# Twelve of 22 feature tiles joint in a macaron block's FFNs; GpSimd splits the last pair's sums; the mixers' first steps come later

## The chip, the cores and the metric

The kernel runs on one core of one Trainium2 chip. The metric is the device time of one execution in microseconds (us). Before the change the median of three runs is 2143.7 us (2139.63 to 2148.18). TensorE (PE) does the matmuls, VectorE (DVE), ScalarE (ACT) and GpSimd (POOL) the elementwise work, SyncE (SP) issues most of the transfers.

## The reference, cut to what matters

The block has 1024 rows of width 1024, all in fp32. Both FFNs have a hidden width of 2816, that is 22 tiles of 128 features.

```python
x = x + 0.5 * _swiglu(_rms_norm(x, ffn1_norm), ffn1_w_gate, ffn1_w_up, ffn1_w_down)
h = _rms_norm(x, mix_norm)
proj = h @ w_in
mixed = concatenate([gla_mixer(proj[:, :GLA_PROJ]), rwkv7_mixer(proj[:, GLA_PROJ:])])
x = x + mixed @ w_out
x = x + 0.5 * _swiglu(_rms_norm(x, ffn2_norm), ffn2_w_gate, ffn2_w_up, ffn2_w_down)
return _rms_norm(x, final_norm)
# _swiglu(h, g, u, d) = (silu(h @ g) * (h @ u)) @ d
```

## The kernel before

The rows are worked on in two halves, A and B, of 512. Every fp32 operand is split into a rounded high part and the rest (`halved`, `stage`, `stage_f`: a cast on ACT, then a subtraction on DVE), and every product is three matmuls: high by high, high by low, low by high (`mm3`). All of them are recorded at line 43; a full one has 512 columns.

**The two kinds of FFN tiles.** Tiles 0 to 11 (`NS` is 12) are done for each half apart in `ffn`: `pgu` is the product with the gate and up weights, `pdn` that with the down weights. Tiles from `NS` on are joint: A and B together, in pairs of tiles, by a scheme with 7 products in place of 8. `joint_up` (`pju`) makes the hidden blocks; at the end of each pair it puts seven operands, named by their product 1 to 7, split, into DRAM (`put`, the transfer at L829). Four of them are sums that GpSimd makes (L833, L835, L838, L842). `joint_down` (`pjd`) then runs the products in the order 1, 6, 2, 7, 5, 4, 3, in each over all pairs. It loads the hidden operand (`hh<-d_hid`), the down weights (`wdk`, loaded with product 1 and kept), forms the weight sums of products 6, 7, 5 and 4 on GpSimd (L864 to L870, into slots of the tile `EG`) and splits them. The results leave PSUM as running sums in the first four slots of `EG` and as additions to the residual rows `x`.

**The order of the stages** is FFN1 of A (tiles per half), joint FFN1, projections and mixers of A, out-projection of A, the same for B, FFN2 of B's first tiles, joint FFN2, final norms and FFN2 of B's other tiles. `mixers` runs the GLA units (`gla_unit`: `pkv`, `pA`, `pB`, `po`) and the RWKV units (`pg`, `p`, `p1b`, `p2b`, `pav`, `pz`, `pu`, `px`, `py`, `pyT`) as streams of small matmuls. Between them it takes fillers from a generator: FFN1 of B beside A's mixers, FFN2 of A beside B's. Each stream yields the nanoseconds from `LAT` that it wants to stay away from PE; it comes back when that has passed in the planner's clock, and for the time placed `FILL` sets how many fillers go in. TensorE's order in there is the one written. The fillers stop at `AFTER`, and what is left of the generator runs as `run(f1b, n=3)` before the out-projection (`pout`) and as `run(f1b)` behind it. The other engines' instructions are ordered by a scheduler at build time.

**Around the change.** Before `pout`, `outprep` loads the mixers' output from DRAM (`xnL<-d_mix`), casts it on ACT (L1285) and subtracts on DVE (L1286). What stands between the last `py` and that: a copy of `py` to `AV` (ACT), a group norm over it (L226 to L233, DVE), a transpose (`pyT`, L46), a scaling (`AV<-pyT`, L244, ACT), an addition and a product (L248, DVE), and the store `d_mix<-AV`.

Of the kernel before, what the change touches and what calls it, by code (L numbers as in the profile page):

```python
# [5 lines left out]
CDEC=float(np.exp(-0.5))  # L6
MULT,ADD,SUB,MAX,MIN=ALU.mult,ALU.add,ALU.subtract,ALU.max,ALU.min

LAT=dict(pre=3000,gram=0,c32=3000,inv2=1400,D=900,m1=900,m2=900,x2=700,pav=900,w=600,z=1000,u=1000,x=1500,gn=6000,gpre=2635,lev0=5723,lev=1944,sc=770,on=8372)

def const_array():
    p=np.arange(128)
# [239 lines left out]
def gla_unit(g, p, src, vsrc, gsrc, mixouts):  # L252
# [10 lines left out]
    fr=[slice(0,64),slice(64,128)]  # L263
    c4=lambda t: t.rearrange("p (c t)->p c t",t=128)
    el=g.el[p]
    yield LAT["gpre"]
    pkv=ps("pkv")
    for c in range(4):
        for h in range(2):
# [83 lines left out]
P = 128  # L353
D = 1024
# [3 lines left out]
DFF = 2816  # L358
NF = DFF // P

NS = 12
PAIRS = [(f, f + 1) for f in range(NS, NF, 2)]
THREES = [list(range(f, min(f + 3, NS))) for f in range(0, NS, 3)]
AFTER = ("gu", len(THREES) - 1, THREES[-1][0])
TWOS = [list(range(f, min(f + 2, NS))) for f in range(0, NS, 2)]
CUT = 6
# [26 lines left out]
def block_kernel(tc, ctx, x, consts, coff, vecs, finaln, wgu, wdn, win_t, win_v, w_out, alw, wa2, g2, out):  # L393
# [300 lines left out]
    def halved(f, H, L):  # L694
        S.copy(H, f)  # L695
        V.tensor_tensor(L, f, H.bitcast(F32), op=SUB)  # L696
# [61 lines left out]
    def joint_up(w, X, ep, spare):  # L758


        def tmp(nm):
            return ep.tile([P, HT], F32, tag="e", bufs=11, name=nm)

        def left(f1, f2, m):

            raw = {(i, kh): stage_load(wgu[w][(f * 2 + m) * 2 + kh]) for kh in range(2) for i, f in ((1, f1), (2, f2))}
            yield 1, stage_f(raw[1, 0])
            s1 = ep.tile([P, HT], F32, tag="s", bufs=3, name="s1")
            GP.tensor_tensor(s1, raw[2, 0], raw[2, 1], op=ADD)
            s2 = ep.tile([P, HT], F32, tag="s", bufs=3, name="s2")  # L770
            GP.tensor_tensor(s2, s1, raw[1, 0], op=SUB)
            yield 6, stage_f(s2)
            yield 2, stage_f(raw[1, 1])
            s3 = ep.tile([P, HT], F32, tag="s", bufs=3, name="s3")
            GP.tensor_tensor(s3, raw[1, 0], raw[2, 0], op=SUB)
            yield 7, stage_f(s3)
            yield 5, stage_f(s1)
            yield 4, stage_f(raw[2, 1])
            GP.tensor_tensor(s2, raw[1, 1], s2, op=SUB)
            yield 3, stage_f(s2)  # L780

        for j, (f1, f2) in enumerate(PAIRS):
            gate, over = {}, {}
            for m in range(2):
                C = {}
                for i, u in left(f1, f2, m):
                    ps = pm.tile([P, HT], F32, tag="pm", name="pju") if i in (6, 7, 4) else pa.tile([P, HT], F32, tag="pa", name="pju")
                    for q in range(4):
                        sl = slice(P * q, P * q + P)
                        xo = (X[i][0][:, q], X[i][1][:, q])  # L790
                        mm3(ps, (u[0][:, sl], u[1][:, sl]), xo, q == 0, q == 3)
                    if i == 1:
                        C[1, 1] = p1 = tmp("p1")
                        S.copy(p1, ps)
                    elif i == 6:
                        C[1, 2] = u2 = tmp("u2")
                        V.tensor_tensor(u2, ps, p1, op=ADD)
                    elif i == 2:
                        V.tensor_tensor(p1, ps, p1, op=ADD)
                    elif i == 7:  # L800
                        C[2, 1] = tmp("u3")
                        V.tensor_tensor(C[2, 1], ps, u2, op=ADD)
                    elif i == 5:
                        C[2, 2] = tmp("c22")
                        V.tensor_tensor(C[2, 2], ps, C[2, 1], op=ADD)
                        V.tensor_tensor(u2, ps, u2, op=ADD)
                    elif i == 4:
                        V.tensor_tensor(C[2, 1], C[2, 1], ps, op=SUB)
                    else:
                        V.tensor_tensor(u2, ps, u2, op=ADD)  # L810
                    for key in {2: [(1, 1)], 5: [(2, 2)], 4: [(2, 1)], 3: [(1, 2)]}.get(i, []):
                        if m == 0:
                            gate[key] = C[key]
                            S.activation(C[key], C[key], AF.Silu)
                        else:
                            V.tensor_tensor(gate[key], C[key], gate[key], op=MULT)

            a11, a12, a21, a22 = gate[1, 1], gate[2, 1], gate[1, 2], gate[2, 2]

            def put(op, f):  # L820
                k = [6, 2, 7, 5].index(op) if j == len(PAIRS) - 1 and op not in (1, 3, 4) else None
                if k is None:
                    hh = ep.tile([P, 2, HT], F32R, tag="hh", bufs=3, name="hh")
                else:
                    if k % 2 == 0:
                        over[k] = spare[0].tile([P, 4, HT], F32R, tag=spare[1][k // 2], name="hhl")
                    hh = over[k // 2 * 2][:, 2 * (k % 2):2 * (k % 2) + 2]
                halved(f, hh[:, 0], hh[:, 1])
                nc.gpsimd.dma_start(hid_dram(w, j, op), hh.bitcast(F32).rearrange("p a t->p (a t)"))  # L829

            put(1, a11)
            s1 = tmp("s1")
            GP.tensor_tensor(s1, a21, a22, op=ADD)  # L833
            s2 = tmp("s2")
            GP.tensor_tensor(s2, s1, a11, op=SUB)  # L835
            put(6, s2)
            put(2, a12)
            GP.tensor_tensor(a11, a11, a21, op=SUB)  # L838
            put(7, a11)
            put(5, s1)  # L840
            put(4, a22)
            GP.tensor_tensor(s2, a12, s2, op=SUB)  # L842
            put(3, s2)

    def joint_down(w, c1, c2, ep, hold, between, first=None, early=False):
# [6 lines left out]
        def right(i, j):  # L852
# [6 lines left out]
            lo0, hi0, lo1, hi1 = kept[j]  # L859
            if i in (1, 2, 3):  # L860
                return stage_f({1: lo0, 2: lo1, 3: hi1}[i])
            t = EG[:, 5 + next(turn) % 3]
            if i == 5:
                GP.tensor_tensor(t, hi0, lo0, op=SUB)  # L864
            else:
# [8 lines left out]
            return [(pa if 4 * k + t < 5 else pm).tile([P, HT], F32, tag="pa" if 4 * k + t < 5 else "pm", name="pjd") for t in range(4)]  # L874

        def sums():
            return ep.tile([P, 8, HT], F32, tag="EG", name="EG")

        turn = iter(range(1000))
        EG = sums() if early else None  # L880
        for i in ORDER:
# [7 lines left out]
                    mm3(ps[t], (hh[:, 0, to], hh[:, 1, to]), u, j == 0, j == n - 1)  # L889
            EG = EG or sums()  # L890
            E = [EG[:, t] for t in range(4)]
            Gs = EG[:, 4]
            for t in range(4):
                def add(x, v, k=0.5):
                    V.scalar_tensor_tensor(x, v, k, x, op0=MULT, op1=ADD)
# [13 lines left out]
                        between[6](E[t][:, 0:1])  # L909
                elif i == 2:  # L910
                    add(x1[:, d1], ps[t])
                elif i == 7:
                    V.tensor_tensor(Gs, ps[t], E[t], op=ADD)
                    add(x2[:, d1], Gs)
                    add(x2[:, d2], Gs)
                    if t == 3 and i in between:
                        between[i](Gs[:, 0:1])
                elif i == 5:
                    add(x2[:, d2], ps[t])
                    add(x1[:, d2], ps[t])  # L920
                    add(x1[:, d2], E[t])
                    if t == 3 and i in between:
                        between[i](x1[:, 0:1])
                elif i == 4:
# [473 lines left out]
    def first(j):  # L1398
        if j < 4 and j % 2 == 0:
            front[j] = B.pool.tile([P, 4, HT], F32R, tag=XN[j // 2], name="hhf")  # L1400
        return front[j // 2 * 2][:, 2 * (j % 2):2 * (j % 2) + 2] if j < 4 else ep.tile([P, 2, HT], F32R, tag="hh", bufs=6, name="hh")

    joint_down(0, A, B, ep, lambda j: wide(A.pool, XN[j]) if j < 4 else wide(ep, "wd"),
               {1: load(A, xsp(A)), 6: load(B, xin(B)), 7: lambda gate: from_store(B, 0, gate), 5: lambda gate: from_store(B, 1, gate)}, first, True)
    from_store_split(B)
    ecm.__exit__(None, None, None)
# [142 lines left out]
```

## Time and profile before

| | |
|---|---|
| median of three runs | 2143.7 us |
| the profiled execution | 2152.21 us |
| its span, first to last instruction | 2150.4 us |
| TensorE busy | 2056.5 us, 96% of the span, 13588 matmuls |
| VectorE, ScalarE, GpSimd busy | 1451.6, 910.6, 469.0 us |
| mean granted TensorE clock | 0.982 |

A matmul on the page is counted busy from its start to its modelled end, and the next one starts before that. So the price of one is the distance of two starts, or the length of a piece in the chain of work that ended last by its count. In brackets behind a row stand the idle time of the engine just before it and what ended it. The profiled execution is 8.5 us above the median.

### The profile page before, as it was taken

The page shows a single profiled execution, that of the slowest core. Times are in us where ns is not written, and L with a number is a line of the kernel's source. Part 1 is how long each engine was busy: PE and PEld are TensorE (multiplying, and loading weights), DVE is VectorE, ACT ScalarE, POOL GpSimd, SP SyncE. Part 2 cuts the span into 40 slices and gives each one's busy share as a digit, 9 for nine tenths or more (in the row PEclk, how much of TensorE's full clock was granted, in tenths as well). Part 3 has the DMA queues.
Part 4 walks back from the last instruction along what each step waited for, and adds up shares of the span by engine and source line. Part 5 has one row for each costly group of instructions (what it writes and reads, how often), then busy time and mean ns, then how long its engine had stood idle before and what let it go on. Part 6 is the DMA issues. An engine that isn't in the chain of part 4 may idle for free. (4 is left out here: it accounts for less than half of the span.)

```text
span 2150.4 us, 36294 instructions
## 1 busy us (share of the span) xinstructions
PE 2056.5 (96%) x13588; PEld 1643.0 (76%) x13588; DVE 1451.6 (68%) x3031; ACT 910.6 (42%) x1703; POOL 469.0 (22%) x490
## 2 busy tenths in 40 slices
PE   8999999978999999999999989999999999988998
PEld 7778788756888777777878867777777878877886
DVE  6675578738659578765575956876668458876755
ACT  6432234322465545354265644535434223432243
POOL 0410364446012300000001220001113036445400
PEclk9999999989999999999999999999999999999999
DMA  5333334676355744324336674442534333459442
GB/s 192 128 118 94 107 133 166 227 274 233 124 196 192 246 136 139 117 81 163 103 123 195 196 254 114 133 119 90 184 101 146 98 103 142 157 192 366 169 139 74
DMA packets 172639, 336.82 MB, mean 157 GB/s; under 512 B 17296, under 2 KB 56240, under 8 KB 172464
## 3 DMA queue, kind: packets, MB, share of 16 engines
q1 hardware_dynamic: 147328, 250.08, 35.9%
q0 software_dynamic: 21536, 73.41, 9.3%
q10 hardware_dynamic: 3600, 11.01, 1.4%
q8 instruction: 107, 1.75, 0.3%
q14 instruction: 68, 0.56, 0.1%
HBM read 242.17 MB, written 92.27 MB: 156 GB/s over the span
## 5 line engine op out<-in xcount | busy, mean ns | idle before, releaser
L460 DVE TENSOR_TENSOR wL<-raw,wH 128x512 fp32r<-128x512 f32 (+1 forms) x430 | 296.5, 697 | 277.7 <-ACT wH L459 275.4
L459 ACT CAST wH<-raw 128x512 fp32r<-128x512 f32 (+1 forms) x430 | 264.2, 619 | 478.2 <-PE pgu L43 161.2
L43 PE MATMUL pgu<-xnH,wH 128*128 128x512 f32 (+1 forms) x784 | 311.8, 398 | 0.1
L43 PE MATMUL pgu<-xnL,wH 128*128 128x512 f32 (+1 forms) x784 | 311.0, 397 | 0.0
L43 PE MATMUL pgu<-xnH,wL 128*128 128x512 f32 (+1 forms) x784 | 309.7, 396 | 0.2 <-DVE wL L460 0.2
L43 PE MATMUL pju<-T,wH 128*128 128x512 f32 x640 | 200.6, 394 | 2.4 <-ACT wH L695 2.4
L43 PE MATMUL pjd<-wH,hh 128*128 128x512 f32 x528 | 169.8, 402 | 24.5 <-ACT wH L695 20.9
L43 PEld LDWEIGHTS pgu<-xnH,wH 128*128 128x128 f32 x784 | 148.6, 190 | 33.5 <-ACT xnH L518 0.5
L43 PEld LDWEIGHTS pgu<-xnH,wL 128*128 128x128 f32 x784 | 148.9, 190 | 33.0 <-DVE wL L460 0.4
L43 PEld LDWEIGHTS pgu<-xnL,wH 128*128 128x128 f32 x784 | 148.9, 190 | 32.5 <-issue 0.7
L43 PE MATMUL pdn<-wH,hH 128*128 128x512 f32 x384 | 155.1, 406 | 6.8 <-ACT silu L665 3.7
L43 PE MATMUL pdn<-wL,hH 128*128 128x512 f32 x384 | 155.7, 406 | 2.4 <-DVE wL L460 2.4
L43 PE MATMUL pdn<-wH,hL 128*128 128x512 f32 x384 | 154.8, 404 | 0.4 <-DVE hL L672 0.4
L631 DVE SCALAR_TENSOR_TENSOR x<-pdn,x 128x512 f32<-128x512 f32 x152 | 104.3, 688 | 65.7 <-PE pdn L43 64.4
L43 PEld LDWEIGHTS pju<-T,wH 128*128 128x128 f32 x640 | 120.2, 188 | 31.1 <-ACT wH L695 3.3
L43 PE MATMUL pp<-xnH,wH 128*128 128x512 f32 x352 | 140.8, 400 | 0.0
L43 PEld LDWEIGHTS pjd<-wH,hh 128*128 128x128 f32 x528 | 101.8, 193 | 49.5 <-ACT wH L695 21.7
L43 PE MATMUL pp<-xnL,wH 128*128 128x512 f32 x352 | 139.0, 395 | 0.0
L43 PE MATMUL pp<-xnH,wL 128*128 128x512 f32 x352 | 138.7, 394 | 0.0
L43 PE MATMUL pju<-T,wL 128*128 128x512 f32 x320 | 126.2, 394 | 0.0
L43 PE MATMUL pjd<-wL,hh 128*128 128x512 f32 x264 | 106.4, 403 | 7.2 <-DVE wL L696 7.2
L696 DVE TENSOR_TENSOR wL<-s,wH 128x512 fp32r<-128x512 f32 x80 | 68.3, 855 | 42.5 <-ACT wH L695 42.5
(395 smaller groups left out, 4127.8 us busy)
## 6 DMA issues: line engine op xcount, KB each, us to landing
raw<-in_wgu_dram SPq DMA_DIRECT2D x272, 256.0 KB, 2.7
hh<-d_hid SPq DMA_DIRECT2D x66, 512.0 KB, 4.6
d_hid<-hh POOLq DMA_DIRECT2D x62, 512.0 KB, 3.7
raw<-in_wdn_dram SPq DMA_DIRECT2D x96, 256.0 KB, 2.6
raw<-in_win_t_dram SPq DMA_DIRECT2D x88, 256.0 KB, 2.9
d_x<-x SPq DMA_DIRECT2D x20, 512.0 KB, 2.9
wdk<-in_wdn_dram SPq DMA_DIRECT2D x20, 512.0 KB, 7.7
raw<-in_w_out_dram SPq DMA_DIRECT2D x32, 256.0 KB, 2.8
```

Source lines behind the costliest of these rows:

```text
L43: return self.t.matmul(out,lhsT,rhs,**kw)
L459: S.copy(H, raw)
L460: V.tensor_tensor(L, raw, H.bitcast(F32), op=SUB)
L631: V.scalar_tensor_tensor(h.x[tt][:, co], ps, 0.5, h.x[tt][:, co], op0=MULT, op1=ADD)
L696: V.tensor_tensor(L, f, H.bitcast(F32), op=SUB)
```

## The change

`NS` goes from 12 to 10, so six pairs (tiles 10 to 21) are joint in both FFNs and ten tiles are done per half. `put` gets another order (1, 2, 4, 6, 7, 5, 3), and for the last pair the four GpSimd sums (6, 7, 5, 3) go to spare tiles and are split by GpSimd itself, with a cast and a subtraction. In `joint_down` `EG` has seven slots in place of eight: the running sum of product 7 is written over the one before it, and its eight additions to `x` come after all four PSUM reads; the additions of product 6's running sum move from product 5 to product 2. In the joint FFN1 the weights of the fifth and sixth pair have tiles of their own. In `LAT`, `pre` goes from 3000 to 8000, and the first GLA unit waits 8000 where it waited 2635. Lines from L829 on move by 4 or 5 (L829 is L833, L866 is L870, L913 is L917).

```diff
-LAT=dict(pre=3000,...,gpre=2635,...)
+LAT=dict(pre=8000,...,gpre=2635,gfirst=8000,...)
...
-    yield LAT["gpre"]
+    yield LAT["gpre" if p else "gfirst"]
...
-NS = 12
+NS = 10
 PAIRS = [(f, f + 1) for f in range(NS, NF, 2)]
-THREES = [list(range(f, min(f + 3, NS))) for f in range(0, NS, 3)]
+THREES = [[0, 1, 2], [3, 4, 5], [6, 7], [8, 9]]
 AFTER = ("gu", len(THREES) - 1, THREES[-1][0])
...
             def put(op, f):
-                k = [6, 2, 7, 5].index(op) if j == len(PAIRS) - 1 and op not in (1, 3, 4) else None
+                k = [6, 7, 5, 3].index(op) if j == len(PAIRS) - 1 and op not in (1, 2, 4) else None
...
-                halved(f, hh[:, 0], hh[:, 1])
+                if k is None:
+                    halved(f, hh[:, 0], hh[:, 1])
+                else:
+                    GP.tensor_copy(hh[:, 0], f)
+                    GP.tensor_tensor(hh[:, 1], f, hh[:, 0].bitcast(F32), op=SUB)
                 nc.gpsimd.dma_start(hid_dram(w, j, op), hh.bitcast(F32).rearrange("p a t->p (a t)"))

             put(1, a11)
+            put(2, a12)
+            put(4, a22)
             s1 = tmp("s1")
             GP.tensor_tensor(s1, a21, a22, op=ADD)
             s2 = tmp("s2")
             GP.tensor_tensor(s2, s1, a11, op=SUB)
             put(6, s2)
-            put(2, a12)
             GP.tensor_tensor(a11, a11, a21, op=SUB)
             put(7, a11)
             put(5, s1)
-            put(4, a22)
             GP.tensor_tensor(s2, a12, s2, op=SUB)
             put(3, s2)
...
-            t = EG[:, 5 + next(turn) % 3]
+            t = EG[:, 4 + next(turn) % 3]
...
-            return ep.tile([P, 8, HT], F32, tag="EG", name="EG")
+            return ep.tile([P, 7, HT], F32, tag="EG", name="EG")
...
-            Gs = EG[:, 4]
...
                 elif i == 2:
                     add(x1[:, d1], ps[t])
+                    add(x1[:, d2], E[t])
                 elif i == 7:
-                    V.tensor_tensor(Gs, ps[t], E[t], op=ADD)
-                    add(x2[:, d1], Gs)
-                    add(x2[:, d2], Gs)
-                    if t == 3 and i in between:
-                        between[i](Gs[:, 0:1])
+                    V.tensor_tensor(E[t], ps[t], E[t], op=ADD)
+                    if t == 3:
+                        for y, e in zip(c2.x, E):
+                            add(y[:, d1], e)
+                            add(y[:, d2], e)
+                        if i in between:
+                            between[i](E[t][:, 0:1])
                 elif i == 5:
                     add(x2[:, d2], ps[t])
                     add(x1[:, d2], ps[t])
-                    add(x1[:, d2], E[t])
...
-    joint_down(0, A, B, ep, lambda j: wide(A.pool, XN[j]) if j < 4 else wide(ep, "wd"),
+    joint_down(0, A, B, ep, lambda j: wide(A.pool, XN[j]) if j < 4 else wide(ep, f"wd{j}"),
```

The order of the instructions shows the rest at three places. On TensorE, at the end of A's mixers, the kernel before has 34 filler matmuls between the last `py` and the transpose `pyT`, and 49 between `pyT` and the first `pout`; around `pyT` they read:

```order
L43 MATMUL pdn<-wH,hH 128x512
L43 MATMUL pdn<-wL,hH 128x512
L46 MATMUL pyT<-ct,AV 128x128 x4
L43 MATMUL pdn<-wH,hL 128x512
L43 MATMUL pgu<-xnH,wH 128x512
```

The changed kernel has at the same place:

```order
L43 MATMUL py<-Xn,AR 64x64 x2
L43 MATMUL py<-UV,W 64x64 x2
L46 MATMUL pyT<-ct,AV 128x128 x4
L43 MATMUL pout_10345<-wH,xnH 128x512
L43 MATMUL pout_10345<-wL,xnH 128x512
```

All 83 fillers have gone from there; the end of B's mixers has changed in the same way. The numbers behind `pout`, `pg`, `s` and `p` are those of buffers.

On TensorE, at the start of A's mixers, 19 `pgu` fillers stand between the projections and the first `pkv` before, the last of them here:

```order
L43 MATMUL pgu<-xnH,wH 128x512
L43 MATMUL pkv<-vN,kN 64x128 x8
L43 MATMUL pgu<-xnL,wH 128x512
L43 MATMUL pgu<-xnH,wL 128x512
L43 MATMUL pg_6779<-AR,BK 128x128
```

Now 56 stand ahead of the first small step, which is `pg`, with `pkv` behind it:

```order
L43 MATMUL pg_7026<-AR,BK 128x128
L43 MATMUL pg_7027<-AR,BK 128x128
L43 MATMUL pkv<-vN,kN 64x128 x8
L43 MATMUL pgu<-xnH,wL 128x512
L43 MATMUL pgu<-xnH,wH 128x512
```

So 37 more fillers are used up at the start (the same in B), and beside each mixer there are 72 fewer in all.

On GpSimd, at the last pair of the joint FFN1, the kernel before has four sums (`s`, `p`) and seven stores (`d_hid`, whose second number is the product):

```order
L829 DMA d_hid_4_1_3754<-hh 128x1024
L829 DMA d_hid_4_4_3782<-hh 128x1024
L829 DMA d_hid_4_2_3767<-hhl 128x1024
L833 TENSOR_TENSOR s_3756<-u_3499,c_3558 128x512
L835 TENSOR_TENSOR s_3758<-s_3756,p_3476 128x512
L838 TENSOR_TENSOR p_3476<-p_3476,u_3499 128x512
L829 DMA d_hid_4_5_3777<-hhl 128x1024
L829 DMA d_hid_4_6_3763<-hhl 128x1024
L829 DMA d_hid_4_7_3773<-hhl 128x1024
L842 TENSOR_TENSOR s_3758<-u_3539,s_3758 128x512
L829 DMA d_hid_4_3_3788<-hh 128x1024
L866 TENSOR_TENSOR EG<-wdk 128x512 x2
```

The changed kernel has, from its second sum on:

```order
L841 TENSOR_TENSOR s_3857<-s_3855,p_3565 128x512
L831 CAST hhl<-s_3855 128x512
L831 CAST hhl<-s_3857 128x512
L843 TENSOR_TENSOR p_3565<-p_3565,u_3588 128x512
L832 TENSOR_TENSOR hhl<-s_3857,hhl 128x512
L831 CAST hhl<-p_3565 128x512
L833 DMA d_hid_5_6_3862<-hhl 128x1024
L832 TENSOR_TENSOR hhl<-p_3565,hhl 128x512
L832 TENSOR_TENSOR hhl<-s_3855,hhl 128x512
L833 DMA d_hid_5_7_3867<-hhl 128x1024
L833 DMA d_hid_5_5_3872<-hhl 128x1024
L846 TENSOR_TENSOR s_3857<-u_3628,s_3857 128x512
```

One more cast and subtraction and the store of product 3 follow, and then the weight sums `EG<-wdk`. Eight instructions have come into GpSimd's queue ahead of those.

## Rows read from the trace of the kernel before

**Rows 1.** The page's busy times: us, share of the span, instructions.

```profile
PE 2056.5 (96%) x13588; PEld 1643.0 (76%) x13588; DVE 1451.6 (68%) x3031; ACT 910.6 (42%) x1703; POOL 469.0 (22%) x490
```

**Rows 2.** The chain that ended last: start us, us, what, how many.

```profile
1521.22 8.07 PE pdn L43 x34
...
1535.52 3.35 DMA d_mix<-AV
1538.93 2.67 DMA xnL<-d_mix
...
1737.21 189.51 PE pju L43 x816
1929.08 11.10 DMA hh<-d_hid
```

**Rows 3.** TensorE's waits over the span: us in total, times, longest.

```profile
PE pjd L43 <- ACT wH L695: 20.9, 2, 11.4
PE pkv L43 <- DMA vN<-d_vn: 15.1, 2, 7.9
```

**Rows 4.** Windows: length, busy us (instructions) of PE, PEld, DVE, ACT, POOL, clock, DMA share, GB/s.

```profile
744.00:757.00 13.00, 5.88 (x31) 4.58 (x31) 4.58 (x11) 4.91 (x7) 1.49 (x2) 0.87 0.96 316
...
1278.00:1291.00 13.00, 5.05 (x27) 3.94 (x27) 4.59 (x11) 4.61 (x7) 0.54 (x1) 0.81 0.95 313
...
1942.00:1957.00 15.00, 15.00 (x60) 12.11 (x60) 9.62 (x8) 3.91 (x7) 13.46 (x10) 0.90 1.03 419
```

**Rows 5.** PE's timeline, ends of both mixers: start us, us, line, operands [idle before].

```profile
992.20 0.60 PE L46 MATMUL pyT<-ct,AV 128*128 128x128 f32 x4
...
1006.05 0.64 PE L43 MATMUL pout<-wH,xnH 128*128 128x512 f32 x1 [1.87 <-ACT xnH L1285]
...
1542.29 0.50 PE L43 MATMUL pout<-wH,xnH 128*128 128x512 f32 x1 [1.15 <-ACT xnH L1285]
```

**Rows 6.** DVE's timeline between the last `py` and `pyT` of A.

```profile
986.35 0.69 DVE L631 SCALAR_TENSOR_TENSOR x<-pdn,x 128x512 f32<-128x512 f32 x1
...
991.33 0.69 DVE L233 TENSOR_TENSOR AV<-AV,vr 128x512 f32<-128x512 f32 x1
```

**Rows 7.** ACT's timeline behind `pyT` of B.

```profile
1529.79 3.73 ACT L244 ACTIVATE AV<-pyT,vt 64x128 f32<-64x128 f32 x8 [0.30 <-PE pyT L46]
```

**Rows 8.** POOL's timeline, last pair of the joint FFN1.

```profile
428.75 1.29 POOL L833 TENSOR_TENSOR s<-u,c 128x512 f32<-128x512 f32 x1
...
431.48 1.61 POOL L838 TENSOR_TENSOR p<-p,u 128x512 f32<-128x512 f32 x1
433.04 0.57 POOL L829 DMA_DIRECT2D d_hid<-hhl  x1
...
448.60 2.48 POOL L866 TENSOR_TENSOR EG<-wdk 128x512 f32<-128x512 f32 x2 [9.75 <-DMA d_hid<-hh]
```

**Rows 9.** PE's timeline, start of product 6 of the joint FFN1.

```profile
453.00 0.80 PE L43 MATMUL pjd<-wH,hh 128*128 128x512 f32 x1 [9.46 <-ACT wH L695]
...
455.57 0.63 PE L43 MATMUL pjd<-wL,hh 128*128 128x512 f32 x1
456.00 0.95 PE L43 MATMUL pjd<-wH,hh 128*128 128x512 f32 x2
```

**Rows 10.** PE's timeline, product 4 of the joint FFN1: its two waits.

```profile
520.01 0.50 PE L43 MATMUL pjd<-wH,hh 128*128 128x512 f32 x1 [3.63 <-DVE EG L913]
533.25 0.80 PE L43 MATMUL pjd<-wL,hh 128*128 128x512 f32 x1 [3.75 <-DVE wL L696]
```

**Rows 11.** DVE's timeline beside that product.

```profile
510.68 3.48 DVE L895 SCALAR_TENSOR_TENSOR x<-EG,x 128x512 f32<-128x512 f32 x2
```

**Rows 12.** ACT's timeline, start of the joint FFN2's down products.

```profile
1939.71 0.62 ACT L695 CAST hh<-s 128x512 fp32r<-128x512 f32 x1 [3.31 <-POOL s L842]
...
1950.06 0.62 ACT L695 CAST wH<-wdk 128x512 fp32r<-128x512 f32 x1 [6.85 <-DMA wdk<-in_wdn_dram]
...
1956.11 0.58 ACT L902 COPY EG<-pjd 128x512 f32<-128x512 f32 x1
```

More of the change, by code (lines that the diff above doesn't have):

```diff
@@ L7 @@
 MULT,ADD,SUB,MAX,MIN=ALU.mult,ALU.add,ALU.subtract,ALU.max,ALU.min
-LAT=dict(pre=3000,gram=0,c32=3000,inv2=1400,D=900,m1=900,m2=900,x2=700,pav=900,w=600,z=1000,u=1000,x=1500,gn=6000,gpre=2635,lev0=5723,lev=1944,sc=770,on=8372)
+LAT=dict(pre=8000,gram=0,c32=3000,inv2=1400,D=900,m1=900,m2=900,x2=700,pav=900,w=600,z=1000,u=1000,x=1500,gn=6000,gpre=2635,gfirst=8000,lev0=5723,lev=1944,sc=770,on=8372)
 def const_array():
```

## The prediction

> **What bounds the kernel now.** I read the page's busy times first: TensorE is busy 96% of the span and the chain that ended last runs mostly through its matmuls [rows 1, 2]. So two things count: how many matmuls there are, and where TensorE stands still. The first has one price. In the chain 816 matmuls of the joint up products took 189.51 us [rows 2], 0.232 us each at the high clock. For the second I read TensorE's waits and then the windows and timelines at each. Two groups of waits are large: 20.9 us before the first operands of the joint down products, once in each FFN, and 15.1 us before `pkv`, the first small step of each mixer [rows 3]. The windows show the latter: 5.88 us busy of 13, and 5.05 of 13, with the transfers at 0.96 and 0.95 of what they can do [rows 4]. The end of the mixers hardly waits: 1.87 us before `pout` in A and 1.15 in B [rows 5], because 83 fillers stand there.
>
> **Matmuls.** A pair done per half takes 2 tiles x 2 halves x (48 `pgu` + 24 `pdn`) = 288; joint it is 7 products x 3 x 12 = 252. Two FFNs save 72, x 0.232 = **-16.7 us**. This has one answer, since all of them are full columns on the engine that sets the end.
>
> **Start of the mixers.** In the order 37 more fillers precede the first small step, 8.6 us; the waits there are 7.9 and 7.2 us [rows 3]. The whole 15.1 us goes, if `vN` lands when it did. The 37 fillers want three more weight tiles of 256 KB through queues that are full [rows 4]; at 316 GB/s that is 2.5 us. If they go ahead of `vN`, each wait keeps 1.7 us or so. I take **-15.1**, between -15.1 and -11. `pkv` no longer has anything queued behind it that waits.
>
> **End of the mixers.** The fillers are not made, they are moved: 72 fewer stand beside each mixer and 37 more at its start, so the last ones are gone. From the last `py` to `pout` nothing is left on TensorE but four transposes. What this uncovers is the length of the chain of small steps, to be read from the rows where fillers now hide it. In B, 8.07 us pass from the last `py` to `pyT` [rows 2]; three filler additions to `x` (L631, 0.69 us each, the first at 986.35 in A [rows 6]) stand in DVE's queue among these steps, and without them I put the stretch at 6.5. Behind `pyT`, ACT scales for 3.73 us from 1529.79 [rows 7], two DVE operations follow, the store takes 3.35, the load 2.67 [rows 2], a cast 0.62 [rows 12]; `pout` starts at 1542.29 [rows 5], 13.1 us after `pyT`, of which a filler's split between the DVE steps is 0.6. That makes 19.0 us of standing still in place of 1.15. In A, `pyT` to `pout` is 13.85 us [rows 5]. Its first loads bring the GLA's output and need not wait for the last store, but sit behind it in SP's queue and took longer. I take 10.4 for this stretch (0.6 + 3.7 + 1.4 + a load of 2.7 to 5 + 0.6), so 16.9 in place of 1.87. Together 17.9 + 15.0 = **+33 us**, 27 if both ends are as short as the pieces, 37 if they last as long as the fillers do today. Between the third `pyT` and the last `py` there are 23 fillers where there were 37; the 14 are 3.3 us a mixer, mostly still hidden: **+2** in all, 0 to 6.
>
> **The clock.** After 9.46 us of standing still the matmuls started 0.43 us apart (455.57, 456.00 [rows 9]), the lower of the two levels, 1.2 GHz; the granted clock was 0.87 and 0.81 in the windows of the mixers' starts [rows 4]. The waits at the start cost some 5 us of slow matmuls in all, and the one in A's end 1.7. The new waits at the ends should cost 2 each, as after 443. **-2.6**, 0 to -6.
>
> **Joint FFN1.** Product 6 waits 9.46 us [rows 9] for its weight sums. POOL, which makes them, stood 9.75 us until a store of `hh` had landed [rows 8]: `EG` lies over that buffer. In the new order the last four operands lie in spare tiles, and the buffers under `EG` are free long before. But POOL's own queue is longer: from 428.75 four sums (1.29 to 1.61, 5.5 in all), four subtractions of the same kind (1.36 each), five stores at 0.55 [rows 8], and four casts. There is no cast on POOL in these rows. ACT takes 0.62 for one [rows 12] and POOL 1.61 for its slowest sum here; I take 1.1. So 5.5 + 5.4 + 2.7 + 4.4 = 18, and POOL starts `EG` at 447 where it was 448.6. TensorE would start at 451.3. Product 1, with a sixth pair (2.8 us), ends at 446.2. The wait is 5.1, that is -4.4; with casts of 0.62 or 1.61, -6.3 or -2.3. On the Trainium skill's page "GPSIMD Engine Reference", section "Engine selection", elementwise work belongs on VectorE: GpSimd is about 2x slower with two inputs and at line rate with one. The first half agrees (1.29 on POOL against 0.69 on DVE [rows 6, 8]) and speaks against the subtractions; by the second the casts would be at ACT's 0.62, an estimate that makes this term 1.9 better.
>
> Product 4 waits 3.63 us for the sums that DVE takes from PSUM one at a time, because each of the four wants the one slot `Gs`, and later 3.75 us for a weight split that stands behind twelve additions [rows 10]. Now the four sums are written in place at once. The eight additions to `x` come behind them, and the last split of product 5 behind these. At 1.74 us each (two took 3.48 [rows 11], while POOL worked) they take 14 us from the end of product 7, and that split is wanted 13.9 us after it; a wait of 0 to 3 us, say 1.5. So -7.4 + 1.5 = -5.9, and -1.5 for the clock, which had fallen there. The page "SBUF — State Buffer" of the Trainium skill, section "Who interferes with whom", says that a DVE operation with two SBUF inputs contends with a GpSimd one that reads SBUF; 1.74 against 0.69 us agrees, and at 0.69 the new wait would be none. The fifth pair's weights now have a tile over an earlier operand's buffer: 0 to +3, I take 1. **FFN1: -11**, between -16 and -5.
>
> **Joint FFN2.** The other half of the 20.9: ACT's weight cast stood behind a cast that waited for POOL (3.31) [rows 12], until 1940. ACT now has no such cast, and the first pair can start near 1930. But the pairs behind it are paced by transfers: a hidden operand took 11.10 us [rows 2], ACT then waited 6.85 for weights [rows 12], and the queues are at 1.03 of their share [rows 4]. The sixth pair's weights lie over the tiles that POOL now still splits; they can be asked for only when its 18 us from 1931 are over, and land near 1955. Product 1's first result was read from PSUM at 1956.1 before [rows 12]; it should be ready near 1957 with a pair more (2.8, counted above). The wait is broken up more than removed: **-2.5**, between -6 and +4.
>
> **The sum.** -16.7 - 15.1 + 33 + 2 - 2.6 - 11 - 2.5 = -12.9. The profiled execution took 2152.2, 8.5 above the median; I apply the difference to the median, 2143.7 - 12.9 = 2131, or -0.6%. About 0.5%, 10.7 us, is what a measurement here can tell from no change. The forecast stands just beyond that.
>
> **Rivals.**
> (a) *The ends of the mixers are shorter*: DVE, ACT, SP and the transfers have no filler work there, and the steps run closer than the rows show; two halves of that chain, 16.9 and 19.0, shrink by a half. For it: the transfers' share. Against it: few fillers' instructions stand between the rows used. -17, so 2114.
> (b) *The joint stages give nothing back*: POOL's casts at 1.6 or more and the late weights hold products 1 and 6 as long as today; the 13.5 us of both stages go. For it: POOL's queue is 10 us longer in both. Against it: TensorE's waits in product 4 have another cause. 2144: no change.
> (c) *Slower, by the clock*: after 17 and 19 us of standing still the clock stays at the lower level for much of `pout`. Each slow matmul costs 0.43 - 0.232 = 0.198 us. `pout` has 192 per half; if both run wholly slow, +76 - 4, so 2203. From 121 slow ones in both it decides: +24 us bring the sum to +0.5%. Against it: after 9.46 us the clock was back within 4 us of work. The rows hold no longer wait.
> (d) *The change doesn't reach the start*: `vN` is late by what the fillers cover, because it is asked for behind their weights. +15, so 2146; the windows' 0.96 speak for it, the order of issue against it.
>
> **How the numbers follow.** The forecast 0.50, (a) 0.12, (b) 0.20, (c) 0.08, (d) 0.10. The forecast's own range by its bounds is 2118 to 2143; just over half of it lies below 2133.0. Faster: 0.27 + 0.12 + 0.06 of (b) and (d) = 0.45. Slower than 2154.4: (c)'s 0.08 and 0.05 of (b) and (d), where ends and joint stages both go wrong, 0.13. Within: 0.42. The range is 2115 to 2152: it leaves out most of (c) and the outer edge of (a).
>
> **What would show it.** Right: 72 matmuls fewer; `pkv` no longer among the waits; new waits before `pyT` and `pout` of 16 to 19 us together in each half; product 6 of FFN1 waiting 3 to 7 us on POOL; no wait on L917; in FFN2 several waits on transfers in place of the 11.4. Wrong: ends under 10 us, or a clock at the lower level through `pout`; POOL casts above 1.7 us; a wait of product 5 over 5 us.

## The result and the profile after

The change made the kernel slower: 2155.32 us (median of seven runs, 2151.69 to 2161.46) against 2143.7 us, a ratio of 1.0059 with a 95% interval of 1.0043 to 1.0075. The forecast was 2131 us, so the sign was wrong, and the time lies outside the range of 2115 to 2152.

The page's head and busy times of the changed kernel, to stand beside [rows 1]:

```profile
span 2155.0 us, 36173 instructions
...
PE 2041.7 (95%) x13516; PEld 1632.1 (76%) x13516; DVE 1457.4 (68%) x3043; ACT 909.9 (42%) x1699; POOL 549.3 (25%) x558
```

The 72 matmuls are gone (13588 to 13516), and TensorE is busy 14.8 us less, yet the span is longer. TensorE's waits over the span, to stand beside [rows 3] (us in total, times, longest):

```profile
PE pout L43 <- ACT xnH L1290: 20.9, 2, 11.4
PE pyT L46 <- DVE AV L233: 16.9, 2, 10.1
PE pjd L43 <- DMA hh<-d_hid: 12.7, 6, 4.0
...
PE pdn L43 <- DVE hf L668: 8.3, 3, 4.9
PE pjd L43 <- DVE wL L696: 6.1, 5, 2.3
```

`pkv` is not among them any more. Where it waited, TensorE now works without a gap, as windows over the end of the projections and the fillers show (length, busy us and instructions of PE, PEld, DVE, ACT, POOL, clock, share of the DMA engines, GB/s); they answer to [rows 4]:

```profile
761.00:776.00 15.00, 15.00 (x88) 12.01 (x87) 8.83 (x20) 6.88 (x11) 0.54 (x1) 1.00 0.98 316
1272.00:1287.00 15.00, 15.00 (x88) 12.05 (x87) 8.51 (x19) 7.03 (x12) 0.54 (x1) 1.00 0.95 311
```

In its place two waits stand at the end of each mixer. TensorE's timeline there, A above and B below (start us, us, in brackets the idle time before and what ended it), beside [rows 5]:

```profile
1003.75 1.09 PE L46 MATMUL pyT<-ct,AV 128*128 128x128 f32 x4 [6.79 <-DVE AV L233]
1014.36 0.79 PE L43 MATMUL pout<-wH,xnH 128*128 128x512 f32 x1 [9.53 <-ACT xnH L1290]
...
1523.30 1.09 PE L46 MATMUL pyT<-ct,AV 128*128 128x128 f32 x4 [10.13 <-DVE AV L233]
1535.80 0.80 PE L43 MATMUL pout<-wH,xnH 128*128 128x512 f32 x1 [11.41 <-ACT xnH L1290]
```

In A the idle time of these two waits is 16.3 us, in B 21.5, where it was 1.87 and 1.15.

**Stage by stage.** I cut each trace where TensorE starts another kind of work. From the difference of a stage's time to that of the kernel before I took 0.2323 us for each full matmul more or fewer, so what is left is time that matmuls don't explain. The kernel before was profiled a second time (below), and its span was 2145.2 us, near its median; the table is made against that trace. All numbers are us.

| kernel | start of the mixers | end, A | end, B | behind `pout` | joint FFN1 | joint FFN2 | matmuls | sum |
|---|---|---|---|---|---|---|---|---|
| changed | -12.1 | +14.8 | +24.5 | +5.9 | -7.2 | +0.3 | -16.7 | +9.5 |
| late start alone | -12.0 | +10.6 | +11.8 | +0.5 | +2.2 | -0.4 | 0 | +12.7 |
| changed, early start | +0.8 | +14.3 | +21.5 | +6.5 | -11.1 | +0.7 | -16.7 | +15.9 |
| joint edits alone | +2.4 | +0.5 | -2.0 | -2.5 | -1.8 | +5.4 | 0 | +2.0 |
| late start, covered | -12.0 | -1.8 | +1.6 | -4.7 | -2.2 | +1.0 | 0 | -18.2 |
| ten tiles, late start, no joint edits | -12.1 | +18.6 | +24.0 | +6.5 | -8.7 | +0.5 | -16.7 | +12.0 |
| before, first trace | +1.0 | -0.7 | +1.1 | +1.6 | +2.2 | 0.0 | 0 | +5.3 |

The last row says how far two executions of one kernel differ: up to 2.2 us in one of these columns, 5.3 in all. "Start" ends at the first `pkv`. Where the mixers start late, `pg` matmuls of 1.1 us in each half stand ahead of that; elsewhere they belong to the next column. "Joint FFN1" holds the FFN1 tiles of A too. The last stage ends with TensorE's last matmul, so the sums can differ from the difference of the spans by 0.3 us.

Beside the mixers and behind `pout` the change takes 4 tiles x 72 = 288 fillers, 66.9 us of matmuls. These stages became only 34 us shorter. The other 33 us (-12.1 + 14.8 + 24.5 + 5.9) are time that the fillers had hidden or that a lower granted clock adds; the experiments tell the two apart in part.

### The profile page after: what moved, and what is told of

The parts are those of the page before. It is cut to its first block, busy times and chain, and to the rows that moved or that the text cites. A ratio compares the mean times of both kernels' runs of the same rounds, so it can differ in the third digit from the quotient of the medians.

```text
span 2155.0 us, 36173 instructions
## 1 busy us (share of the span) xinstructions
PE 2041.7 (95%) x13516; PEld 1632.1 (76%) x13516; DVE 1457.4 (68%) x3043; ACT 909.9 (42%) x1699; POOL 549.3 (25%) x558
## 3 DMA queue, kind: packets, MB, share of 16 engines
q0 software_dynamic: 23552, 80.76, 10.4%
## 4 chain that ended last, share of the span: by engine, by line
PE 81%; DVE 8%; DMA 4%; issue 2%; ACT 2%; POOL 2%; SPq 0%; ACTq 0%; DVEq 0%; POOLq 0%
PE pju L43 21%; PE pgu L43 17%; PE pp L43 11%; PE pdn L43 10%; PE pjd L43 7%; PE pout L43 4%; PE pv L43 2%; PE po L43 1%; PE py L43 1%; DVE wL L460 1%; DVE x L898 1%; DMA hh<-d_hid 1%; DVE T L696 1%; PE ptn L46 1%; PE pt L46 1%
## 5 line engine op out<-in xcount | busy, mean ns | idle before, releaser
L459 ACT CAST wH<-raw 128x512 fp32r<-128x512 f32 (+1 forms) x382 | 233.6, 618 | 376.7 <-PE pgu L43 118.8
L43 PE MATMUL pgu<-xnH,wH 128*128 128x512 f32 (+1 forms) x656 | 259.4, 397 | 0.3 <-ACT xnH L518 0.2
L43 PE MATMUL pgu<-xnL,wH 128*128 128x512 f32 (+1 forms) x656 | 258.8, 396 | 0.0
L43 PE MATMUL pgu<-xnH,wL 128*128 128x512 f32 (+1 forms) x656 | 258.4, 395 | 0.0
L43 PE MATMUL pju<-T,wH 128*128 128x512 f32 x768 | 240.7, 394 | 2.4 <-ACT wH L695 2.4
L43 PE MATMUL pjd<-wH,hh 128*128 128x512 f32 x640 | 207.1, 403 | 13.1 <-DMA hh<-d_hid 12.7
L43 PEld LDWEIGHTS pjd<-wH,hh 128*128 128x128 f32 x640 | 123.7, 193 | 45.0 <-issue 14.3
L43 PE MATMUL pju<-T,wL 128*128 128x512 f32 x384 | 151.4, 394 | 0.0
L43 PE MATMUL pdn<-wL,hH 128*128 128x512 f32 x320 | 129.3, 404 | 0.8 <-DVE wL L460 0.8
L43 PE MATMUL pdn<-wH,hL 128*128 128x512 f32 x320 | 129.0, 403 | 1.2 <-DVE hL L672 1.2
L696 DVE TENSOR_TENSOR wL<-s,wH 128x512 fp32r<-128x512 f32 x96 | 98.9, 1032 | 29.3 <-ACT wH L695 29.3
L631 DVE SCALAR_TENSOR_TENSOR x<-pdn,x 128x512 f32<-128x512 f32 x144 | 98.5, 686 | 28.9 <-PE pdn L43 27.8
```

The lines of the kernel that those rows point to most:

```text
L43: return self.t.matmul(out,lhsT,rhs,**kw)
L459: S.copy(H, raw)
L631: V.scalar_tensor_tensor(h.x[tt][:, co], ps, 0.5, h.x[tt][:, co], op0=MULT, op1=ADD)
```

## The experiments

Two theories stand against each other. *The place of the fillers decides*: the mixers are a chain of small steps with a length of its own; fillers that are taken away, or used up at the start, uncover it. *The joint stage decides*: GpSimd's longer queue and the six pairs cost what the matmuls save. The medians of the kernel before in the three sets of runs were 2145.9, 2145.3 and 2146.9 us; each ratio below is to the kernel before in the same set.

**The kernel before once more.**

> The kernel before, unchanged, profiled a second time. Theory 'the trace was typical': the waits before the joint down products (9.5 and 11.4 us) and the two at product 4 (3.6, 3.8 us) come back within 1 us each, and the execution takes about 2152 us. Rival 'the traced execution was a long one': some of these waits are shorter by 8 us together, and the execution takes about 2144 us.

It took 2146.9 us with its profile, and the span is 2145.2. TensorE's waits:

```profile
PE pjd L43 <- ACT wH L695: 21.7, 2, 11.4
PE pkv L43 <- DMA vN<-d_vn: 14.1, 2, 7.1
...
PE pjd L43 <- DVE wL L696: 6.3, 3, 3.0
PE pout L43 <- ACT xnH L1285: 4.1, 2, 2.4
```

The waits before the joint down products and before `pkv` are typical. The wait of 3.6 us on L913 [rows 10] isn't in this trace at all; in the covered run below it is 2.1 us. So the first trace was a long one by 5.3 us, spread thinly, and one of the waits that the forecast removed isn't there every time.

**Late start alone.**

> The kernel before with the two numbers of LAT alone (pre 8000, first GLA unit 8000); 12 tiles per half as before. Now 56 fillers precede each mixer and 44 of the 83 are left at its end. Theory 'fillers are only moved': the two waits before pkv go (-15 us, and -3 of slow matmuls), and the 39 fillers missing at each end uncover 9 us a half, so +18: 2141 to 2149 us, waits before pyT and pout of 9 to 11 us a half. Rival 'the end is covered anyway': -15 us or more, 2129 us.

```diff
-LAT=dict(pre=3000,...,gpre=2635,...)
+LAT=dict(pre=8000,...,gpre=2635,gfirst=8000,...)
...
-    yield LAT["gpre"]
+    yield LAT["gpre" if p else "gfirst"]
```

2156.43 us, ratio 1.0042 (1.0026 to 1.0058): slower, and by more than was expected. The waits:

```profile
PE pout L43 <- ACT xnH L1285: 20.2, 2, 10.8
```

`pkv` has gone from the list and `pout` has come in with 20.2 us. The start gave 12 us, the two ends took 22 (table). 39 fillers fewer at each end are 9.1 us a half. Between the last `py` and `pout`, where they are missing, they cost 7.9 us in A and 8.8 in B. The other 2.7 and 3.0 us stand ahead of the last `py`, where a stretch at the lower clock, shown with the seventh run, costs 4.4 us in each half. So the late start of this kernel moves a wait from the start to the end, and the lower clock comes on top. Of the ten executions three took 2147.8 to 2149.7 us at a mean granted clock of 0.984 or 0.985, about as the theory wanted, and seven 2154.6 to 2160.6 us at 0.978 or 0.979; the traced one is of the seven.

**The changed kernel with the early start.**

> The changed kernel with LAT as before, so the mixers begin behind 19 fillers. Theory 'fillers are only moved': TensorE's order has no filler at the ends in this one either, so the ends wait 17 and 19 to 22 us as in the changed kernel, and the waits before pkv (15 us) come back on top: 2165 to 2172 us. Rival 'the late start is what costs': the ends get cover back and the time falls to about 2143 us.

The edit sets `pre` back to 3000 and `gfirst` to 2635. 2165.45 us, ratio 1.0096 (1.0081 to 1.0111), as the first theory wanted:

```profile
PE pout L43 <- ACT xnH L1290: 21.1, 2, 11.4
PE pyT L46 <- DVE AV L233: 15.8, 2, 9.0
PE pkv L43 <- DMA vN<-d_vn: 14.9, 2, 7.6
```

All three waits stand together. With 576 fillers beside the mixers there are none left for the ends, wherever the mixers start, and here the late start saves some 8 us (ratio 1.0096 to 1.0059). So it isn't the late start that made the changed kernel slow; it softens what the ten tiles do.

**The joint stage's edits alone.**

> The kernel before with the edits of the joint stage alone (new order and GpSimd's splits in put, sums in place, seven slots), with five pairs and LAT as before. Theory 'stalls of the joint stage go': product 4 of FFN1 waits under 1 us in place of 7.4, product 6 waits 3 to 5 us less; in FFN2 the 11.4 us become 8 to 14 us of waits on transfers: 2128 to 2138 us. Rival 'the joint stage gives nothing back': 2142 to 2146 us.

The edit is that of the diff in `joint_up` and `joint_down`, with `NS = 12`. 2146.67 us, ratio 1.0002 (0.9990 to 1.0015): no change, the rival was right.

```profile
PE pjd L43 <- DVE wL L696: 16.3, 7, 4.4
...
PE pjd L43 <- ACT wH L695: 6.9, 2, 6.5
PE pjd L43 <- DMA hh<-d_hid: 5.7, 3, 2.8
```

The 11.4 us before FFN2's product 1 are gone, and waits for weight splits and hidden operands have come, 28.9 us together; in the second trace of the kernel before the first and third of the rows shown are 28.0. FFN1 gained 1.8 us and FFN2 lost 5.4 (table).

**Late start, covered.** Fillers that stood behind `pout`, where the norm needs only a few of them, come ahead of it.

> The kernel before with the two numbers of LAT (pre and the first GLA unit 8000) and one more unit of fillers taken from behind pout to ahead of it: run(f1b, n=4) and run(f2a, n=4) in place of n=3. The order then has 56 fillers at the start of the mixers, 31 before pyT and 61 between pyT and pout (before: 34 and 49). Theory 'the place of the fillers decides': waits before pkv gone (-13 us), waits before pyT and pout under 4 us a half, 0 to 4 us lost behind pout: 2130 to 2138 us beside 2146 for the kernel before. Rival 'a late start costs something of its own': 2143 us or more.

```diff
-    run(f1b, n=3)
+    run(f1b, n=4)
...
-    run(f2a, n=3)
+    run(f2a, n=4)
```

This is on top of the late start, with twelve tiles and the joint stage as before. 2130.14 us, ratio 0.9934 (0.9921 to 0.9946): the fastest kernel here. What the ends wait for is at the bottom of the list:

```profile
PE pout L43 <- ACT xnH L1285: 0.8, 1, 0.8
PE pyT L46 <- DVE AV L233: 0.4, 2, 0.2
```

The same matmuls as before, the same late start that alone costs 0.4%, and 48 fillers per half in another place: by the ratios 1.1%, some 23 us, lie between these two kernels. In the traces 4.4 us of the difference are the stretch at the lower clock, which stands in both halves there and in B alone here. Against the kernel before, late start and move together gain 0.66%, some 14 us. The second theory has no part in that.

**The last pair's splits on ACT and DVE again.**

> The changed kernel with the last pair's four sums split by ACT and DVE again (all else as changed). Theory 'GpSimd's splits only move the wait': ACT stands behind GpSimd's sums again, so the joint FFN2 has one wait of 8 to 12 us before product 1 in place of five of 1 to 4, and the joint stages together take within 4 us of the changed kernel's: 2151 to 2159 us. Rival 'GpSimd's longer queue eats the gain': product 6 and the sixth pair come 5 us earlier in both FFNs, 2143 to 2149 us.

```diff
-                if k is None:
-                    halved(f, hh[:, 0], hh[:, 1])
-                else:
-                    GP.tensor_copy(hh[:, 0], f)
-                    GP.tensor_tensor(hh[:, 1], f, hh[:, 0].bitcast(F32), op=SUB)
+                halved(f, hh[:, 0], hh[:, 1])
```

2157.46 us, ratio 1.0055 (1.0037 to 1.0072), not to be told from the changed kernel's 1.0059.

```profile
PE pjd L43 <- ACT wH L695: 11.1, 1, 11.1
...
PE pjd L43 <- DMA hh<-d_hid: 7.0, 1, 7.0
```

The wait in one piece is back, and the joint stages together lose nothing by it: by the cut of the table they are 4.2 us shorter than the changed kernel's, while the ends of the mixers are 8.7 us longer, with two stretches at the lower clock that the changed kernel's trace hasn't. These runs see no difference by who splits the last pair's sums.

**GpSimd held back at the end of B's mixers.** In the trace of the changed kernel B's end stands still for 5 us longer than A's. VectorE's timeline there, and GpSimd's below:

```profile
1511.64 2.92 DVE L201 TENSOR_TENSOR Xe<-Xt,pc 128x256 f32<-128x256 f32 x1
1514.48 0.67 DVE L226 TENSOR_REDUCE sm<-AV 128x8 f32<-128x512 f32 x1
1515.19 2.65 DVE L227 TENSOR_SCALAR sm<-sm 128x8 f32<-128x8 f32 x1
```

```profile
1511.78 2.49 POOL L717 TENSOR_TENSOR xs<-xnH,xnL 128x512 f32<-128x512 f32 x2
1514.21 1.09 POOL L718 DMA_DIRECT2D d_xf<-xs  x2
1515.32 2.48 POOL L717 TENSOR_TENSOR xs<-xnH,xnL 128x512 f32<-128x512 f32 x2
```

A step over 128x8 elements takes 2.65 us, from 1515.19 to 1517.84, and GpSimd's two additions end at 1517.80. They are half A's normed rows on their way to DRAM.

> The changed kernel, in which GpSimd's eight additions xs (L717, half A's normed rows on their way to DRAM) wait until the out-projection's first operand of half B is cast, by a one-column copy ahead of each. Theory 'two small DVE steps at the end of B's mixers (2.92 and 2.65 us in place of 0.42 and 0.17) stand still while GpSimd adds': they fall to 0.4 and 0.2, last py to pyT in B from 10.35 to 6.5 to 7.1 us, and the subtraction for pout takes up to 3.7 us as it did before the change; 1 to 4 us faster than the changed kernel. Rival 'something else holds DVE there': still 9 to 10 us.

```diff
-    def to_store(h):
+    def to_store(h, gate):
         for kt in range(8):
             t = t2("xs")
+            GP.tensor_copy(t[:, 0:1], gate)
...
-    to_store(A)
+    to_store(A, B.xh(0)[:, 0:1].bitcast(F32))
```

VectorE's timeline at the same place, without GpSimd beside it:

```profile
1512.25 0.42 DVE L201 TENSOR_TENSOR Xe<-Xt,pc 128x256 f32<-128x256 f32 x1
1514.31 0.69 DVE L226 TENSOR_REDUCE sm<-AV 128x8 f32<-128x512 f32 x1 [1.64 <-ACT AV L208]
1515.03 0.17 DVE L227 TENSOR_SCALAR sm<-sm 128x8 f32<-128x8 f32 x1
```

The two steps fell from 2.92 to 0.42 and from 2.65 to 0.17 us, as expected, and B's end in the trace from +24.5 to +19.6. 2152.31 us, ratio 1.0033 (1.0018 to 1.0047): 0.26% or some 5 us below the changed kernel's 1.0059, though the intervals touch. Both traces have the stretch at the lower clock in B, so it has no part in that difference.

**A stretch at the lower clock.** A's end was 4 us longer in this trace than in the changed kernel's, and also in those of the two kernels with the old splits and the old joint stage, though A's code up to there is the same. The clock explains it. Between the first and the second `pyT` of a mixer stand 32 `po` matmuls with 15 `pdn` behind them. Windows over these 47, in the changed kernel's A and B and then in this run's A:

```profile
881.10:891.40 10.30, 10.27 (x47) 7.47 (x47) 4.70 (x12) 2.29 (x4) 0.00 (x0) 1.00 0.26 78
1390.75:1405.45 14.70, 14.68 (x47) 10.53 (x47) 4.79 (x12) 2.27 (x4) 0.00 (x0) 0.65 0.16 55
...
877.75:892.50 14.75, 14.71 (x47) 10.55 (x47) 4.82 (x12) 2.30 (x4) 0.00 (x0) 0.65 0.19 55
```

TensorE is busy throughout in all three, and as many matmuls of the same kinds take 4.4 us longer where the granted clock is 0.65 (a mean of the higher level and of some 10 us at the lower one, 0.5). Just ahead of the `po` TensorE stands still for 0.6 us, which the profile puts down to nothing ("issue"), in every trace with the late start and in none with the early start. Of the 16 mixers traced with the late start 12 have the stretch, of the eight with the early start none. The pause alone doesn't decide, since four mixers have it without the stretch; what does is open.

**Ten tiles and the late start, without the joint edits.**

> Ten tiles per half, six joint pairs and the late start, but the joint stage's code as before (old order in put, splits on ACT and DVE, eight slots, one sum at a time); only the fifth and sixth pair's weights have tiles of their own. Theory 'the joint edits move waits': mixers as in the changed kernel (ends 17 and 22 us); product 6 of FFN1 waits 8 to 11 us, FFN2's product 1 8 to 12 us in one piece: 2152 to 2162 us. Rival 'six pairs need the edits': 2165 us or more.

2163.09 us, ratio 1.0087 (1.0068 to 1.0106), just above what the theory wanted and below the rival.

```profile
PE pout L43 <- ACT xnH L1285: 21.8, 2, 11.3
PE pyT L46 <- DVE AV L233: 16.9, 2, 10.1
PE pjd L43 <- ACT wH L695: 11.0, 1, 11.0
PE pjd L43 <- DMA hh<-d_hid: 7.7, 1, 7.7
```

The waits at the ends are those of the changed kernel. The expected wait of product 6 in FFN1 isn't there: with six pairs product 1 is longer, and the wait that remains is one for transfers. FFN1 is 8.7 us shorter here without the edits, against 7.2 with them (table): the gain there comes with the sixth pair. Whether the edits are worth the 0.3% by which this kernel is slower isn't settled: its trace puts them at 2.5 us, less than the 4.4 us that the lower clock takes in its A, and with five pairs they were worth nothing.

**Ten tiles, with their last fillers ahead of `pout`.** This is the edit of the covered run, on the changed kernel.

> The changed kernel with run(f1b, n=4) and run(f2a, n=4): the last 48 fillers, which stand behind pout in the changed kernel, come ahead of it; 41 of them then stand between the last py and pyT, none between pyT and pout and none behind pout, where the next norm waits for the rows. Theory 'with ten tiles there are too few fillers, wherever they stand': the wait before pyT goes (-7 and -9 us), the waits before pout stay at 9.5 to 11.5, and the norm behind pout waits 4 to 9 us more in each half: within 6 us of the changed kernel, 2149 to 2159 us. Rival 'only their place was wrong': 2140 us or less, as with twelve tiles.

2152.46 us, ratio 1.0031 (1.0019 to 1.0043).

```profile
PE pout L43 <- ACT xnH L1290: 21.0, 2, 11.3
...
PE ptn L46 <- DVE xs L549: 10.1, 5, 3.8
...
PE pyT L46 <- DVE AV L233: 2.7, 2, 2.0
```

The wait before `pyT` fell from 16.9 to 2.7 us, and the stages behind `pout` lost 12 (from +5.9 to +17.8 by the same cut), where the norm's `ptn` now stands uncovered. The edit that is worth some 23 us with twelve tiles is worth some 6 with ten (1.0059 to 1.0031). In none of the three arrangements tried with ten tiles (early start, late start, this one) are there enough fillers.

**Twelve tiles, covered, with the joint edits.**

> Twelve tiles per half, the late start, one more unit of fillers ahead of pout (as in the covered run), and the joint stage's edits with five pairs. Theory 'the joint edits move waits': FFN1 3 to 5 us shorter, FFN2 4 to 6 us longer, in all within 4 us of the covered run without them: 2127 to 2134 us. Rival 'the edits gain on their own': 2125 us or less.

2130.57 us, ratio 0.9938 (0.9922 to 0.9954), against 0.9934 without the edits. They add nothing here either. The three parts are now told apart. Ten tiles cost what they uncover at the ends, the late start gains or costs by whether fillers are left for the ends, and the joint edits are worth nothing that these runs can tell with five pairs.

## Why the prediction was wrong

Most of the waits were named, and the sign of the sum was wrong. It was small beside its terms (47.9 us of gains against 35 of loss), and five of them missed in the same direction. The steps that failed are these. The stages behind `pout` were put at nothing and took 5.9 us. B's end took 24.5 us for 17.9: GpSimd's additions beside VectorE's steps and the stretch at the lower clock had no term. The start and the clock gave 12.1 us for 17.7. And the edits of the joint stage, priced at 13.5 us in both FFNs, gave nothing that these runs can tell; 6.9 us came off there, and 8.2 without the edits (the row of the table with the late start and no joint edits), so the gain came with the sixth pair. Point by point, forecast against the table:

- **Matmuls, -16.7.** Right as a count. As a saving it is only true where nothing hides behind the matmuls; what they hid is in the next points.
- **Start of the mixers, -15.1 and part of the clock's -2.6.** Measured -12.1; the `pg` that now stand ahead of `pkv` take 2.2 us of it, so the waits went as forecast (-14.3). The 5 us of slow matmuls that the clock's term gives back here don't show: between the first `pkv` and the second `pyT`, where the clock was low behind the waits, A is 0.3 us shorter and B 2.9 us longer, because the late start has brought the stretch at the lower clock to B.
- **End of A, +15.0.** Measured idle 6.79 + 9.53 us, forecast 6.5 and 10.4; as a stage +14.8, where A had no stretch at the lower clock; in the three other traces with ten tiles in which it had one the stage is 4 us longer. This reading, the chain taken from rows where fillers hide it, held to the microsecond.
- **End of B, +17.9.** Measured +24.5, of which 19.6 lie between the last `py` and `pout` and 4.9 ahead of that. From `pyT` on the forecast of 12.5 was right (1523.30 to 1535.80). The stretch from `py` to `pyT` was not: 10.13 us of idle time where I had 6.5, because GpSimd's additions stand in VectorE's way there; with them held back it is 6.8. The stretch at the lower clock accounts for 4.4 of the 4.9 us. Nothing in the rows that I chose showed GpSimd's queue at that place; in the kernel before they began at 1543.7, behind the first `pout` of B.
- **Behind `pout`, nothing.** This is the step that I left out. I counted 72 fillers fewer beside each mixer, and didn't ask what the 72 fewer behind `pout` had covered. Measured +5.9 us, and 6.5 in the two other kernels with ten tiles in the table. The largest new wait there is in B, for VectorE's product `hf` in FFN2 of B's tiles, which was 0.8 us in the kernel before:

```profile
1646.28 0.80 PE L43 MATMUL pdn<-wH,hH 128*128 128x512 f32 x1 [4.90 <-DVE hf L668]
```

The norm's transposes wait 1.9 us in both halves together where they waited 0.9. That the fillers had covered the wait for `hf` isn't shown: with still fewer of them behind `pout`, in the ninth run, it is 0.8 us and the norm waits 9.7.

- **Joint FFN1, -11.** Measured -7.2, with the kernel before's own scatter of 2.2 between two traces. GpSimd's casts were 0.6 us, not 1.1:

```profile
436.75 1.17 POOL L831 CAST hhl<-s 128x512 fp32r<-128x512 f32 x2
```

This is two casts in 1.17 us. The Trainium skill's page "GPSIMD Engine Reference", section "Engine selection", has one-input operations of GpSimd at about line rate, and the trace agrees: by its estimate the term would have come out better than I took it. What held TensorE was another thing, transfers of hidden operands within product 1: for its first pair, its fifth and its sixth. I had put 1 us, for the fifth pair's weights:

```profile
433.57 0.47 PE L43 MATMUL pjd<-wH,hhf 128*128 128x512 f32 x1 [2.67 <-DMA hhf<-d_hid]
450.42 0.47 PE L43 MATMUL pjd<-wH,hh 128*128 128x512 f32 x1 [3.96 <-DMA hh<-d_hid]
456.78 0.47 PE L43 MATMUL pjd<-wH,hh 128*128 128x512 f32 x1 [1.79 <-DMA hh<-d_hid]
```

Product 6 follows at 461.0 without any wait. It has none in the kernel without the joint edits either, where a wait of 7.75 us for the fifth pair's operand stands in product 1: product 1, longer by the sixth pair and by that wait, outlasts the weight sums, and the wait that the edits were to remove had gone already. And of the 7.4 us at product 4 one half isn't there in every execution.

- **Joint FFN2, -2.5.** Measured +0.3, inside the bounds. The single wait became several for transfers, as forecast:

```profile
1958.10 0.47 PE L43 MATMUL pjd<-wH,hh 128*128 128x512 f32 x1 [1.15 <-DMA hh<-d_hid]
...
1969.47 0.47 PE L43 MATMUL pjd<-wH,hh 128*128 128x512 f32 x1 [3.96 <-DMA hh<-d_hid]
```

- **The clock, -2.6.** Rival (c) was wrong. After 9.53 us of standing still `pout` starts slowly and is at the high level 3.5 us later (starts 0.43 us apart, then 0.23):

```profile
1014.95 0.63 PE L43 MATMUL pout<-wL,xnH 128*128 128x512 f32 x1
1015.38 0.63 PE L43 MATMUL pout<-wH,xnL 128*128 128x512 f32 x1
...
1018.14 0.40 PE L43 MATMUL pout<-wH,xnH 128*128 128x512 f32 x1
1018.38 0.40 PE L43 MATMUL pout<-wL,xnH 128*128 128x512 f32 x1
```

What the term lacks is the stretch at the lower clock beside a busy TensorE.

The misses against the sum: start and clock 5.6 (the clock's -2.6 is inside the stages), ends 4.3 (39.3 for 35), behind `pout` 5.9, FFN1 3.8, FFN2 2.8, together 22.4 of the 22.4 between the forecast -12.9 and the table's +9.5. That the forecast was made from one trace, 5.3 us longer than the next, made the waits look a little more worth removing than they are.

Rival (b), that the joint stages give nothing back, had the edits' worth right, as far as the joint edits alone show it with five pairs, and not the reason: GpSimd's casts took 0.6 us, not 1.6, and product 6 didn't wait. Its 2144 us is short by 11. Rivals (a) and (d) fell: the ends didn't shrink, and the start was reached, so that (d)'s 2146, the nearest of the rivals' times, is near by luck. The forecast's list of what would show it held for the matmuls, for `pkv`, for A's end (16.3 us), for L917 and for the waits on transfers in FFN2; B's end was longer (21.5 us for 16 to 19), and product 6 didn't wait on POOL. Its range was too narrow: it had no room for the stages behind `pout`, and the bounds of the terms were put together as if they missed independently.

## What to carry to other kernels

Where matmuls stand as fillers beside a chain of dependent steps, a scheme that saves matmuls by taking them from there saves only those that hid nothing: here 34 of 66.9 us came off, and the matmuls of the sixth pair were paid in full in the joint stages. Before filler work is removed, moved or used up earlier, write down for every place that loses some what it covered there, behind the stage as well as in it; and look for filler that stands where nothing needs it. 48 matmuls a half, moved from behind the out-projection to ahead of it, were worth some 23 us beside the late start alone, more than the 16.7 us of the matmuls that the change saves. And a wait seen in one execution should be looked for in a second one before its removal is put into a sum; so should the granted clock of a stretch before a difference of two traces is put down to the code.

## What the hardware showed that I had not expected

A VectorE step over 128x8 elements, 0.17 us by itself, took 2.65 us while GpSimd made two additions, and ended 0.04 us after them; a 128x256 step went from 0.42 to 2.92 us. With GpSimd held back both were short again. The Trainium skill's page "SBUF — State Buffer", section "Who interferes with whom", says that VectorE and GpSimd share a pair of ports, that whoever is first holds it for the whole instruction and the other fully blocks, and that `tensor_scalar` can be among those that want it. The trace agrees that the step lasts until GpSimd is through, and here it lasted through two GpSimd instructions in a row (2.48 us together). It doesn't show who was first: VectorE's two steps begin 0.13 and 0.14 us ahead of GpSimd's additions in it.

TensorE's granted clock fell to the lower level for some 10 us while it worked, behind a pause of only 0.6 us, in 12 of 16 mixers with the late start; 47 matmuls took 14.7 us there in place of 10.3.
